# Cutting the tail of a streaming row-maximum into loads of graded size

## The chip, the cores and the metric

The kernel runs on one core of one Trainium2 chip. One execution in profile gives a span that is about 1.8 us shorter than its time (628.1 against 629.88 us for the kernel before).

## The reference

For each row of an 8192 x 8192 float32 matrix, the largest absolute value:

```python
def setup_inputs():
    return {"x": np.random.randn(8192, 8192).astype(np.float32)}

def reference(x):
    return np.linalg.norm(x, ord=np.inf, axis=1)
```

The input is 268.4 MB and the output 32 KB. Every element is read once and compared once, so the kernel is a stream from DRAM into on-chip memory with one reduction behind it.

## The kernel before

The rows are spread over 128 partitions, 64 rows to a partition. The first 48 rows are the bulk: 24 loads of two rows (16,384 columns, 8.4 MB) into three rotating buffers, each followed by one VectorE reduction. The last 16 rows are the tail: eight buffers of two rows, cut into smaller loads so that the reduction behind the last byte is short.

```python
TAIL = (
    [[8192]] * 8
    + [[4096, 4096]] * 5
    + [[2048] * 4] * 2
    + [[2048, 2048, 2048, 1024, 512, 512]]
)
# ...
    for a in range(A):                       # bulk
        for n in range(G):
            t = sbuf.tile([P, B * cols + 16], F32, tag="t")
            nc.sync.dma_start(out=t[:, : B * cols], in_=x_b[a, n])
            absmax(r_bulk[:, a, n * B : (n + 1) * B], ...)
    nc.scalar.dma_start(out=out_b, in_=r_bulk[:])      # the bulk store
# ...
            for k, w in enumerate(TAIL[r]):  # tail, row by row
                nc.sync.dma_start(
                    out=t[:, at : at + w], in_=x_t[i // B][:, at : at + w]
                )
                # ... one absmax per load, into part[:, r, k] or behind the buffer
```

All loads are issued by SyncE. The last load's reduction reads its own columns and, behind them in the buffer, the partial results of the last row (517 columns in all); its result goes out with the last small DMA.

## Time and profile before

| Kernel before | value |
|---|---|
| time, median | 629.97 us (three runs: 629.9 to 630.3; with three more 630.14) |
| input stream | 427 GB/s over the span, 434 GB/s in the bulk (loads of 8.4 MB land 19.28 to 19.37 us apart, 19.33 in the mean) |
| last bulk tile landed / its reduction ended | 467.46 / 484.7 us |
| last byte landed | 623.50 us |
| VectorE ended | 625.74 us, 2.23 us after the last byte |
| rest (result DMA, closing barrier) | 2.36 us |

The groups of instructions of the kernel before (page part 5: busy us, mean ns of one | idle before it, and what ended that):

```profile
L63 DVE TENSOR_REDUCE r_bulk<-t 128x2 f32<-128x16384 f32 x24 | 413.3, 17219 | 70.5 <-DMA t<-in_x_dram 70.5
L63 DVE TENSOR_REDUCE part<-t 128x1 f32<-128x4096 f32 (+2 forms) x26 | 130.0, 5067 | 1.3 <-DMA t<-in_x_dram 1.3
...
L63 DVE TENSOR_REDUCE r_fin<-t 128x1 f32<-128x517 f32 x1 | 0.7, 692 | 0.0
```

In the bulk VectorE waits 70.5 us for loads (17.22 us of work per 19.33 us of stream). In the tail it waits only 1.3 us before the 26 of its 32 reductions that this line counts (1.7 us in all): it comes in 17 us behind, because it may begin the last bulk tile only when that has landed, and has to catch up. It can, but slowly: a column costs VectorE 1.0416 ns (reductions of 8,192 and 4,096 columns start 8.60 and 4.33 us apart), and the stream brings one every 1.19 ns (loads of 8,192 columns land 9.72 us apart).

The end of the kernel before in the timeline (start us, us, engine, line, operation, output<-input, count, in brackets the idle time before it):

```profile
615.96 0.22 DVE L63 TENSOR_REDUCE r_tail<-part 128x15 f32<-128x60 f32 x1
616.09 2.28 DVE L63 TENSOR_REDUCE t<-t 128x1 f32<-128x2048 f32 x1
616.21 0.35 ACTq L88 DMA_DIRECT2D out_dram<-r_tail  x1
618.52 2.29 DVE L63 TENSOR_REDUCE t<-t 128x1 f32<-128x2048 f32 x1 [0.15 <-DMA t<-in_x_dram]
621.01 4.01 DVE L63 TENSOR_REDUCE t<-t 128x1 f32<-128x2048 f32 x3 [0.20 <-DMA t<-in_x_dram]
625.05 0.69 DVE L63 TENSOR_REDUCE r_fin<-t 128x1 f32<-128x517 f32 x1
625.77 0.35 SPq L99 DMA_DIRECT2D out_dram<-r_fin  x1
```

VectorE waits for the last load of 2,048 columns until 621.01. The bytes behind it (1,024 + 512 + 512 columns) are all there by 623.50, but from 621.01 VectorE still has 2,048 + 1,024 + 512 + 517 columns to reduce and is done at 625.74. So here the small last load does not make a short end, because a load three places before it is large.

Last, SyncE's own waits and one DMA line of the kernel before (us in total, times, longest; then KB and us from issue to landing):

```profile
SPq L82 <- DMA t<-in_x_dram: 65.5, 21, 4.6
...
SPq L82 <- DMA out_dram<-r_bulk: 23.2, 1, 23.2
```

```profile
out_dram<-r_bulk ACTq DMA_DIRECT2D x1, 24.0 KB, 57.9
```

A load is carried by 16 DMA engines, eight packets each, and sends one completion from each of them (the trace has 128 packets and 16 completions for each load); "ring" means the row of packets of one queue on one engine. The loads share eight rotating semaphores with the other DMAs (numbers 100 to 107 in the trace), so each waits for the DMA eight places before it. One of those is the store of the bulk result: 24 KB, but 57.9 us from issue to landing. One load waits 23.2 us for it. That costs nothing here, since the stream still has loads queued: the store lands at 542.66 us, and the loads issued by then last to 550.06.

### The profile page before, as it was taken

How to read it: one execution, taken by the hardware profiler on the slowest of the kernel's cores; microseconds unless marked ns; L12 is line 12 of the kernel's file. 1: busy time of each engine (PE TensorE's matmuls, PEld its weight loads, DVE VectorE, ACT ScalarE, POOL GpSimd, SP SyncE). 2: the span in 40 equal slices, each digit the busy share in tenths (PEclk: the TensorE clock that was granted, in tenths of full speed). 3: DMA queues.
4: the chain of work that ended last, by engine and by line, in shares of the span. 5: the costliest groups of instructions: out<-in, count | busy, mean ns of one | idle time of the engine just before them, and what ended most of it. 6: DMA issues, size and time to landing. Idle time of an engine off the chain costs nothing.

```text
span 628.1 us, 196 instructions
## 1 busy us (share of the span) xinstructions
DVE 552.7 (88%) x58; POOL 0.2 (0%) x4
## 2 busy tenths in 40 slices
DVE  0588988889988889888898888998889999999998
POOL 0000000000000000000000000000000000000000
DMA  9999999999999999999999999999999999999996
GB/s 401 413 455 413 455 413 455 413 455 413 455 413 455 409 459 413 455 413 455 413 455 413 455 413 455 413 455 413 455 405 430 434 435 432 420 432 432 424 426 274
DMA packets 9138, 268.49 MB, mean 427 GB/s; under 512 B 1968, under 2 KB 1968, under 8 KB 2352
## 3 DMA queue, kind: packets, MB, share of 16 engines
q1 hardware_dynamic: 8208, 268.44, 99.1%
q10 hardware_dynamic: 928, 0.03, 0.1%
q14 instruction: 2, 0.02, 0.0%
HBM read 268.44 MB, written 0.03 MB: 427 GB/s over the span
## 4 chain that ended last, share of the span: by engine, by line
DMA 64%; DVE 30%; another core or an unknown queue 4%; issue 1%; SPq 0%
DMA t<-in_x_dram 64%; DVE r_bulk L63 23%; DVE part L63 5%; DVE t L63 1%; SPq L82 0%; DVE r_fin L63 0%; SPq L68 0%
## 5 line engine op out<-in xcount | busy, mean ns | idle before, releaser
L63 DVE TENSOR_REDUCE r_bulk<-t 128x2 f32<-128x16384 f32 x24 | 413.3, 17219 | 70.5 <-DMA t<-in_x_dram 70.5
L63 DVE TENSOR_REDUCE part<-t 128x1 f32<-128x4096 f32 (+2 forms) x26 | 130.0, 5067 | 1.3 <-DMA t<-in_x_dram 1.3
L63 DVE TENSOR_REDUCE t<-t 128x1 f32<-128x2048 f32 (+2 forms) x5 | 8.6, 1746 | 0.4 <-DMA t<-in_x_dram 0.4
L60 DVE MEMSET part<- 128x60 f32 x1 | 0.1, 108 | 0.8 <-PEq L114 0.8
L63 DVE TENSOR_REDUCE r_fin<-t 128x1 f32<-128x517 f32 x1 | 0.7, 692 | 0.0
L63 DVE TENSOR_REDUCE r_tail<-part 128x15 f32<-128x60 f32 x1 | 0.2, 216 | 0.0
L114 POOL MEMSET const-bfloat16-1.0<- 128x1 bf16 x1 | 0.1, 101 | 0.0
L114 POOL MEMSET const-uint8-127<- 128x1 uint8 x1 | 0.1, 101 | 0.0
L114 POOL MEMSET const-float32-0.0<- 128x1 f32 x1 | 0.1, 98 | 0.2 <-issue 0.2
L114 POOL MEMSET const-float32-1.0<- 128x1 f32 x1 | 0.1, 98 | 0.0
## 6 DMA issues: line engine op xcount, KB each, us to landing
t<-in_x_dram SPq DMA_DIRECT2D x8, 4096.0 KB, 37.0
t<-in_x_dram SPq DMA_DIRECT2D x10, 2048.0 KB, 30.4
t<-in_x_dram SPq DMA_DIRECT2D x11, 1024.0 KB, 24.6
t<-in_x_dram SPq DMA_DIRECT2D x1, 512.0 KB, 15.9
t<-in_x_dram SPq DMA_DIRECT2D x2, 256.0 KB, 13.2
t<-in_x_dram SPq DMA_DIRECT2D x24, 40.7
out_dram<-r_bulk ACTq DMA_DIRECT2D x1, 24.0 KB, 57.9
out_dram<-r_tail ACTq DMA_DIRECT2D x1, 7.5 KB, 5.6
```

The source lines that it names most:

```text
L60: nc.vector.memset(part[:], 0.0)
L63: nc.vector.reduce_max(out=o, in_=i, axis=X, apply_absolute_value=True)
L114: nc = _bacc.Bacc("TRN2", target_bir_lowering=False, num_devices=1)
```

## The change

The tail is cut into loads of graded size. In the last two buffers each is mostly 0.83 to 0.95 of the one before it; in the earlier ones large and small loads mix (those of each buffer add up to 16,384 columns). A load may span the boundary of two rows (its two pieces are then reduced separately). The ratio to aim at is 0.88, the quotient of VectorE's and the stream's time per column (1.0416 and 1.19 ns): each load should be reduced just while the next arrives, down to a last load of 1,024 columns. Core of the diff:

```diff
-TAIL = (
-    [[8192]] * 8
-    + [[4096, 4096]] * 5
-    + [[2048] * 4] * 2
-    + [[2048, 2048, 2048, 1024, 512, 512]]
-)
+TAIL = [
+    [2944, 13440],
+    [4096, 12288],
+    [11520, 4864],
+    [7680, 8704],
+    [6528, 3328, 6528],
+    [4864, 4096, 3328, 4096],
+    [3968, 3584, 3328, 2944, 2560],
+    [2432, 2176, 1920, 1664, 1536, 1280, 1152, 1024, 1152, 1024, 1024],
+]
# ... segments() cuts each load at the row boundary; the loop now goes load by load:
+        for j, w in enumerate(loads):
+            nc.sync.dma_start(out=t[:, at : at + w], in_=x_t[i][:, at : at + w])
+            at += w
+            for _, b, c, n in [s for s in todo if s[0] == j]:
+                # ... absmax of this piece, as before
```

Loads in the tail go from 32 to 31, reductions on loaded data from 32 to 38. Bulk, buffers and bytes stay.

More of the change, by code (lines that the diff above doesn't have):

```diff
@@ L13, with segments @@
 X = mybir.AxisListType.X
-TAIL = (
-    [[8192]] * 8
-    + [[4096, 4096]] * 5
-    + [[2048] * 4] * 2
-    + [[2048, 2048, 2048, 1024, 512, 512]]
-)
+TAIL = [
[8 more added lines that the diff above has]
+]
+def segments(loads, cols):
+    out, at = [], 0
+    for i, w in enumerate(loads):
+        end = at + w
+        while at < end:
+            r = at // cols
+            to = min(end, (r + 1) * cols)
+            out.append((i, r, at - r * cols, to - at))
+            at = to
+    return out
 @with_exitstack
@@ L33 @@
     BUFS: int = 3,
+    PAD: int = 16,
 ):
@@ L37 @@
     rows, cols = x.shape
-    n_tail = len(TAIL)
-    assert n_tail % B == 0
+    W = B * cols
+    n_tail = B * len(TAIL)
     n_bulk_rows = rows // P - n_tail
@@ L52 @@
     outp = ctx.enter_context(tc.tile_pool(name="outp", bufs=1))
-    k_last = len(TAIL[-1])
+    segs = [segments(loads, cols) for loads in TAIL]
+    count = {}
+    for i, s in enumerate(segs):
+        for _, r, _, _ in s:
+            count[i * B + r] = count.get(i * B + r, 0) + 1
+    n_last = count[n_tail - 1]
+    k_max = max(count[r] for r in range(n_tail - 1))
+    assert n_last - 1 <= PAD
     r_bulk = outp.tile([P, A, G * B], F32)
@@ L57 @@
     r_fin = outp.tile([P, 1], F32)
-    k_max = max(len(r) for r in TAIL[:-1])
     part = outp.tile([P, n_tail - 1, k_max], F32)
@@ L66 @@
         for n in range(G):
-            t = sbuf.tile([P, B * cols + 16], F32, tag="t")
-            nc.sync.dma_start(out=t[:, : B * cols], in_=x_b[a, n])
+            t = sbuf.tile([P, W + PAD], F32, tag="t")
+            nc.sync.dma_start(out=t[:, :W], in_=x_b[a, n])
             absmax(
                 r_bulk[:, a, n * B : (n + 1) * B],
-                t[:, : B * cols].rearrange("p (b c) -> p b c", b=B),
+                t[:, :W].rearrange("p (b c) -> p b c", b=B),
             )
     nc.scalar.dma_start(out=out_b, in_=r_bulk[:])
-    for i in range(0, n_tail, B):
-        t = sbuf.tile([P, B * cols + 16], F32, tag="t")
-        for j in range(B):
-            r = i + j
-            at = j * cols
-            last = r == n_tail - 1
-            for k, w in enumerate(TAIL[r]):
-                nc.sync.dma_start(
-                    out=t[:, at : at + w], in_=x_t[i // B][:, at : at + w]
-                )
-                if last and k == k_last - 1:
-                    absmax(r_tail[:, : n_tail - 1], part[:])
-                    nc.scalar.dma_start(
-                        out=out_t[:, : n_tail - 1], in_=r_tail[:, : n_tail - 1]
-                    )
-                    absmax(r_fin[:], t[:, at : B * cols + k_last - 1])
-                elif last:
-                    absmax(
-                        t[:, B * cols + k : B * cols + k + 1], t[:, at : at + w]
-                    )
-                else:
-                    absmax(part[:, r, k : k + 1], t[:, at : at + w])
-                at += w
@@ new lines @@
+    seen = {}
+    for i, loads in enumerate(TAIL):
+        t = sbuf.tile([P, W + PAD], F32, tag="t")
+        todo = segs[i]
+        at = 0
+        for j, w in enumerate(loads):
+            nc.sync.dma_start(out=t[:, at : at + w], in_=x_t[i][:, at : at + w])
+            at += w
+            for _, b, c, n in [s for s in todo if s[0] == j]:
+                r = i * B + b
+                k = seen.get(r, 0)
+                seen[r] = k + 1
+                lo = b * cols + c
+                if r < n_tail - 1:
+                    absmax(part[:, r, k : k + 1], t[:, lo : lo + n])
+                    if r == n_tail - 2 and k == count[r] - 1:
+                        absmax(r_tail[:, : n_tail - 1], part[:])
+                        nc.scalar.dma_start(
+                            out=out_t[:, : n_tail - 1], in_=r_tail[:, : n_tail - 1]
+                        )
+                elif k < n_last - 1:
+                    absmax(t[:, W + k : W + k + 1], t[:, lo : lo + n])
+                else:
+                    absmax(r_fin[:], t[:, lo : W + n_last - 1])
```

## The prediction

> **What bounds the kernel now.** The input stream. The page gives 268.4 MB at 427 GB/s; the DMA row is 9 in 39 of 40 slices. In the trace, loads of 16,384 columns land 19.37 us apart (433 GB/s) and tail loads of 8,192 every 9.72 us. [...] So only what follows the last byte can go.
>
> **The end of before (timeline).** The last bulk tile lands at 467.46 us and its 17.22 us reduction ends at 484.6, so VectorE enters the tail 17 us behind. Reductions of 8,192, 4,096 and 2,048 columns start 8.60, 4.33 and 2.20 us apart: 1.0416 ns a column plus about 0.06 us. The stream brings a column every 1.19 ns, so VectorE gains 12% and just catches up over the 156 us of the tail (idle there: 1.7 us). The last landings: 620.98 (2,048 columns), 622.27 (1,024), 622.90 and 623.50 (512 each). VectorE does 2,048, 1,024, 512 and 517 columns after 620.98 and ends at 625.74, 2.24 us after the last byte. The result's DMA and the barrier take 2.36 us more.
>
> **What the change does.** Bulk, bytes and buffers stay. Tail loads go from 32 to 31, reductions in the tail from 32 to 38 (loads that span rows need two): 6 x 0.06 = 0.4 us more VectorE work. The ratio 0.88 is the two rates' quotient (1.0416/1.19 = 0.875): each load is reduced just while the next arrives. With the trace's rates I get landings of the last three loads (1,152, 1,024, 1,024) at about 621.1, 622.3 and 623.5, VectorE starting the last at 623.6 and ending at about 624.8. The same sum for before gives 625.6 (measured 625.74).
>
> Stream: a packet costs about 8 ns plus its bytes (8 KB 309 ns, 32 KB 1213 ns, 64 KB 2418 ns), so other sizes cost it nothing.
>
> **Issue waits.** Eight load semaphores rotate, and one slot is held by the bulk result's store, which takes 57.9 us: 48 small packets per ring, each apparently alternating with one load packet (48 x 1.21 = 58). [...] After the change I expect it to land near 543 again, with the stream filled to about 553: no bubble. Later loads wait for the eighth before, with about 10 us of stream left.
>
> **On the critical path:** only the end after the last byte, 2.24 us to about 1.3 us. That is 0.9 us, 0.15%.
>
> **Predicted:** 629.1 us, 8 in 10 between 628.5 and 629.9. Faster by over 2%: 0.003; within 2%: 0.992; slower: 0.005.
>
> **What would show each step.** Last byte at 623.5 +- 0.4 from the span's start; VectorE ends 1.2 to 1.5 us after it; r_fin's reduction reads about 1,034 columns and is busy 1.2 us; VectorE idles about 1.2 us in the tail, mostly before the 12,288 and 11,520 loads; the bulk store takes 55 to 60 us and the stream has no hole after it.
>
> **What would make it wrong.** Loads of odd widths (11,776 or 53,760 bytes a row) streaming slower than 27 bytes/ns per engine: 1% over the tail is 1.6 us, more than the gain. VectorE not having caught up at the end because early large loads make it wait longer than I sum. Or a store landing 10 us later, which would drain the stream.

## More of the kernel before

The metric is the device time of one execution in microseconds (us), the median of the fast runs.

The page of the kernel before, parts 2 and 3 (in the DMA row a digit is the busy share of one of 40 slices in tenths; a queue's line has packets, MB and its share of the 16 engines' time):

```profile
DMA  9999999999999999999999999999999999999996
...
DMA packets 9138, 268.49 MB, mean 427 GB/s; under 512 B 1968, under 2 KB 1968, under 8 KB 2352
...
q1 hardware_dynamic: 8208, 268.44, 99.1%
...
q14 instruction: 2, 0.02, 0.0%
```

The stream is busy in every slice but the last: it is what bounds the kernel.

## The result, and the profile after

| | before | after |
|---|---|---|
| time, median of 6 runs | 630.14 us (629.9 to 630.55) | 629.40 us (629.15 to 629.86) |
| last bulk tile landed | 467.46 us | 467.59 us |
| last byte landed | 623.50 us | 623.99 us |
| stream from last bulk tile to last byte | 156.04 us | 156.40 us |
| VectorE ended | 625.74 us | 625.42 us |
| ... after the last byte | 2.23 us | 1.43 us |
| rest | 2.36 us | 2.29 us |
| span of the profiled run | 628.1 us | 627.7 us |

The ratio is 0.9988 with a 95% interval of 0.9975 to 1.0001: the same within 2%, and the times alone do not settle that it is faster. (A ratio is the mean time of one kernel's runs over that of the other's of the same rounds, so it is not quite the ratio of the medians quoted. Executions over 1.5% slower than the fastest of the same kernel are left out of the means.) The traces tell more than the times here, and they show two things that go against each other: the end after the last byte became 0.80 us shorter, and the last byte came 0.49 us later.

The page of the kernel after, the lines that answer to those of before:

```profile
DMA packets 8994, 268.49 MB, mean 428 GB/s; under 512 B 1952, under 2 KB 1952, under 8 KB 3104
...
q14 instruction: 2, 0.02, 0.0%
...
L88 DVE TENSOR_REDUCE part<-t 128x1 f32<-128x8192 f32 (+18 forms) x31 | 130.4, 4273 | 0.9 <-DMA t<-in_x_dram 0.6
L88 DVE TENSOR_REDUCE t<-t 128x1 f32<-128x1152 f32 (+3 forms) x6 | 7.9, 1386 | 0.0
L88 DVE TENSOR_REDUCE r_fin<-t 128x1 f32<-128x1030 f32 x1 | 1.2, 1225 | 0.0
```

The end of the kernel after in the timeline:

```profile
614.21 1.88 DVE L88 TENSOR_REDUCE part<-t 128x1 f32<-128x1664 f32 x1
616.12 0.22 DVE L88 TENSOR_REDUCE r_tail<-part 128x15 f32<-128x60 f32 x1
616.25 7.91 DVE L88 TENSOR_REDUCE t<-t 128x1 f32<-128x1536 f32 x6
...
624.19 1.23 DVE L88 TENSOR_REDUCE r_fin<-t 128x1 f32<-128x1030 f32 x1
625.44 0.35 SPq L126 DMA_DIRECT2D out_dram<-r_fin  x1
```

No bracket stands behind any of these lines: VectorE works without a visible pause to the end, and only one reduction of 1,030 columns (1.23 us) lies behind the last byte, where before there was a piece of a large one and three small ones. The bulk store and the wait for it (SyncE's waits, then the DMA line):

```profile
SPq L106 <- DMA out_dram<-r_bulk: 25.0, 1, 25.0
```

```profile
out_dram<-r_bulk ACTq DMA_DIRECT2D x1, 24.0 KB, 60.0
```

The store lands at 544.9 us, the loads queued by then last to 553.0 us, so no hole opens.

Where did the 0.49 us of the last byte come from? 0.13 us were there when the tail began. In the tail, landing by landing, the rest is made up by one step: the load of 4,096 columns that ends the sixth tail buffer took 5.31 us to land after the one before it, where such a load took 4.80 to 4.98 us in the kernel before. The packet records of the trace show why that load is late: one of its 128 packets of 16,384 bytes took 1,251 ns, where their median is 611 ns. Right before it, at 579.58 us, an 8,192-byte packet of the instruction queue (q14) had taken 309 ns, and the slow packet began at its end, at 579.89. The same happens once more at 593.62 us (a packet of 912 ns where the median is 498), but no load lands late there. In the kernel before, one such pair lies in the stream (588.35 us), and the second q14 packet comes only at 626.95, when the stream is over.

The late load also reaches the end. Lines of the timeline of the kernel after, then of the chain of work that ended last (start us, us, what):

```profile
520.12 95.96 DVE L88 TENSOR_REDUCE part<-t 128x1 f32<-128x8192 f32 x25 [0.64 <-DMA t<-in_x_dram]
```

```profile
556.97 40.73 DMA t<-in_x_dram
597.70 0.02 issue
597.72 18.37 DVE part L88 x8
```

VectorE's one long wait is that of 0.64 us. But its reductions at 589.43, 593.73 and 597.72 also begin within 0.03 us of a landing, after waits that are too short for a bracket, and the chain runs over the stream up to the landing at 597.70. Reductions that wait for nothing overlap by 0.08 us in this trace; measured by that, the three waits add up to about 0.4 us (an estimate), nearly the 0.44 us by which the load that landed at 584.66 us was late (5.31 us less the 4.87 of the mean such load in the kernel before).

### The profile page after: what moved, and what is told of

The parts are those of the page before. It is cut to its first block, busy times and chain, and to the rows that moved or that the text cites. A ratio compares the mean times of both kernels' runs of the same rounds, so it can differ in the third digit from the quotient of the medians.

```text
span 627.7 us, 201 instructions
## 1 busy us (share of the span) xinstructions
DVE 553.0 (88%) x64; POOL 0.2 (0%) x4
## 4 chain that ended last, share of the span: by engine, by line
DMA 67%; DVE 28%; another core or an unknown queue 4%; SPq 0%; issue 0%
DMA t<-in_x_dram 67%; DVE r_bulk L88 22%; DVE part L88 5%; DVE t L88 1%; DVE r_fin L88 0%; SPq L106 0%; SPq L93 0%; DVE r_tail L88 0%
## 5 line engine op out<-in xcount | busy, mean ns | idle before, releaser
L88 DVE TENSOR_REDUCE part<-t 128x1 f32<-128x8192 f32 (+18 forms) x31 | 130.4, 4273 | 0.9 <-DMA t<-in_x_dram 0.6
L88 DVE TENSOR_REDUCE t<-t 128x1 f32<-128x1152 f32 (+3 forms) x6 | 7.9, 1386 | 0.0
```

Source lines behind the costliest of these rows:

```text
L88: nc.vector.reduce_max(out=o, in_=i, axis=X, apply_absolute_value=True)
```

## The experiments

Two questions. First, what makes the end after the last byte: the sizes in the last tail buffer alone, the grading of the whole tail, or only the size of the last load? Second, what delays the last byte: the unequal sizes, or the instruction queue's packets, and is there any danger from the bulk store? Each kernel is the changed kernel with one edit, except where "the tail of before" is named (its sizes written in the changed kernel's table). All gave the correct result. The four sessions were on four chips, and each ran the kernel before alongside; its median was 629.87 to 630.42 us. The table has the profiled run of each; "fetches" counts 8-KB packets of the instruction queue between the span's start and the last byte.

| kernel | last bulk tile to last byte | VectorE's end after last byte | fetches | span of that run | time, median |
|---|---|---|---|---|---|
| before | 156.04 | 2.23 | 1 | 628.10 | 630.14 |
| after | 156.40 | 1.43 | 2 | 627.71 | 629.40 |
| after_again | 156.53 | 1.44 | 2 | 628.47 | 629.48 |
| last_only | 156.30 | 1.72 | 1 | 628.36 | 629.53 |
| first_seven | 156.35 | 2.21 | 2 | 628.43 | 630.02 |
| unaligned | 156.99 | 1.28 | 2 | 628.54 | 629.92 |
| fine_end | 156.50 | 1.48 | 2 | 627.86 | 629.49 |
| more_code | 156.22 | 1.48 | 10 | 632.38 | 633.78 |
| store_two | 159.28 | 1.44 | 2 | 630.75 | 632.36 |
| store_small | 161.16 | 1.43 | 2 | 632.50 | 634.28 (one run) |
| before_more | 156.47 | 2.20 | 2 | 628.60 | 630.36 |
| rows_graded | 156.04 | 1.73 | 1 | 627.60 | 629.81 |
| two_issuers | 156.06 | 1.75 | 0 | 630.32 | 632.53 |
| rows_better | 156.70 | 1.45 | 1 | 628.03 | 629.81 |

### The change again (after_again)

No edit.

> The changed kernel as it is, to see what repeats. Theory A (the gain is the shorter end after the last byte, and single slow packets in the stream take part of it back at random): VectorE again ends 1.2 to 1.5 us after the last landing, against 2.24 us before; the load of 4,096 columns that took 5.31 us at 579 to 585 us takes 4.87 us this time; time 0.5 to 1.0 us below the kernel before. Rival (the unequal loads themselves stream slower at that place): the same load takes about 5.3 us again.

The end after the last byte repeated (1.44 us). But my theory of the day, that the late load was chance, fell: the same load was late again (last byte of that buffer 20.12 us after the one before it, 19.96 the first time, 19.54 in the kernel before), again with one packet of 16,384 bytes at 1,260 ns, behind a packet of the instruction queue. The load is late for a reason that is in the program. The rival, that the sizes themselves stream slower there, was still open. Time 629.48 against 629.87 us of the kernel before, 0.4 us less where 0.5 to 1.0 was expected; the ratio of 0.9995 (0.9982 to 1.0007) does not show that it is less.

### Only the last tail buffer graded (last_only), only the first seven (first_seven)

```diff
 # last_only: seven buffers as before, then
+    [2432, 2176, 1920, 1664, 1536, 1280, 1152, 1024, 1152, 1024, 1024],
 # first_seven: seven graded buffers, then
+    [2048, 2048, 2048, 2048, 2048, 2048, 2048, 1024, 512, 512],
```

> Seven tail tiles as before, only the last tile cut in the graded way (11 loads from 2,432 to 1,024). Theory A: what the grading of the last tile alone gives is the whole gain. In the trace of before VectorE starts the last tile at 607.07 us, in that after the change at 607.22, so from there it should end at 625.3 us, 1.2 to 1.6 us after the last byte, time 0.5 to 1.0 us below before. Rival (the grading has to run through the whole tail for VectorE to be caught up): VectorE enters the last tile late and ends 2 us or more after the last byte, no gain.

> The graded loads in the first seven tail tiles, the last tile as before (2,048 x 7, 1,024, 512, 512). Theory A: VectorE ends 2.1 to 2.4 us after the last byte as before, time within 0.3 us of before. Rival (whole grading): most of the gain is here, 1.2 to 1.6 us after the last byte, 0.5 us or more faster.

The end after the last byte is 2.23 us with neither, 2.21 with the first seven alone, 1.72 with the last alone and 1.43 with both. So the grading of the first seven buffers gains nothing by itself, the last buffer gives 0.5 of the 0.8 us, and the other 0.3 us need both. Theory A of last_only was right in direction but too strong: it asked for at most 1.6, and for a time 0.5 to 1.0 us below before, where 0.3 was measured. The reason is in VectorE's pauses: in the tail it idles 1.62 us in last_only and 0.96 us in the changed kernel, where it waits for loads of 8,192 and 4,096 columns in the middle of the tail. Theory A of first_seven held (2.21 us; time 0.15 us above before). The times point the same way: 629.53 us for last_only, 630.02 for first_seven, against 629.87 for the kernel before (intervals 0.9984 to 1.0009 and 0.9989 to 1.0016, so the order among them is shown by the traces and not by the times).

### A finer end (fine_end)

```diff
-    [2432, 2176, 1920, 1664, 1536, 1280, 1152, 1024, 1152, 1024, 1024],
+    [2432, 2176, 1920, 1664, 1536, 1280, 1152, 1024, 896, 768, 640, 512, 384],
```

> The changed kernel with the last eight loads cut finer (896, 768, 640, 512, 384 in place of 1,152, 1,024, 1,024; 13 loads in the last tile for 11). Theory G (VectorE works without a pause from the landing of the 11,520 load at 520 us on, so its whole remaining work sets the end, and each further load adds 0.06 us to it): VectorE ends 0.1 to 0.2 us later than with the change, 140.7 to 141.0 us after it began the tail, and time is the same within 0.3 us. Rival (what follows the last byte is the last load's own reduction): the end after the last byte falls from 1.43 us to about 0.6 us and the time by 0.7 us.

The rival is refuted: it asked for about 0.6 us after the last byte. Theory G held in its numbers, though not in its reason. The last reduction is now much shorter (its group in the page of fine_end):

```profile
L88 DVE TENSOR_REDUCE r_fin<-t 128x1 f32<-128x392 f32 x1 | 0.6, 561 | 0.0
```

Yet VectorE ends 1.48 us after the last byte (1.43 with the change), 140.82 us after it began the tail (140.67 and 140.81), and the time is 629.49 us. (The 0.1 to 0.2 us that Theory G asked for two more loads are no more than two runs of the change differ by, so that cost is not shown.) VectorE is not without a pause from 520 us on, as the theory had it: its last wait of note ends with the landing at 597.70 us in the changed kernel and at 597.52 in fine_end. From there to 625.42 us (625.36) it is fed without a visible gap, so what sets its end is all the work it has left at that landing, and a smaller last load only moves where it is queued. Grading and VectorE's rate are one limit: with 12% to spare, no load may be larger than about 14% of the columns that follow it (an estimate from the two measured rates, 1.19/1.0416 - 1, which no run tests by itself), apart from what one lets stand at the end.

### Boundaries off the grid (unaligned)

```diff
-    [2944, 13440],
+    [2977, 13407],
 # ... likewise +33/-33 columns in every tail buffer
```

> The changed kernel with nearly all inner load boundaries moved by 33 columns (132 bytes), so that neither the rows in DRAM nor those in SBUF start on a multiple of 256 bytes. Theory A (a packet costs about 8 ns plus its bytes whatever its size and start): stream and time as in after_again within 0.3 us. [...]

The stream of the tail took 156.99 us against 156.40 and 156.53, so 0.5 us more; time 629.92 us, 0.4 us more. That is over the 0.3 us of Theory A, so it did not hold as it stands. The packets show little: where the changed kernel's 13,312-byte packets had a median of 498 ns, here they had 500, and those of 16,004 to 16,516 bytes took 604 to 616. That is up to 3 ns more for most sizes, 8 for the worst. So starts on the grid are worth keeping here, but for half a microsecond. It also answers the rival of after_again in part: sizes and starts matter far less than the one late packet of 0.6 us.

### More code on an idle engine (more_code)

```diff
+    idle = outp.tile([P, 1], F32)
+    for _ in range(1024):
+        nc.gpsimd.memset(idle[:], 0.0)
```

> The changed kernel with 1,024 one-column memsets on the idle GpSimd engine at its start (about 100 ns each, nobody waits for them). It tests what the runs so far suggest: in every trace the one late packet of a slow tail load begins right after an 8,192-byte packet of the instruction queue, at the same instruction each time. Theory F (each instruction fetch of 8 KB takes its place in one ring of the 16, puts that ring about 0.7 us behind for the rest of the stream, and the last byte waits for the slowest ring): the instruction queue shows 7 to 9 packets more inside the span, the last byte comes 0.7 us (all on different rings) to 6 us (all on one ring) after 624.3, and the time follows. Rival (fetches are hidden, the late loads have another cause): last byte at 624.0 to 624.7 us as in the changed kernel, time within 0.3 us of it.

633.78 us, 4.3 us slower than the change, ratio to the kernel before 1.0063 (1.0051 to 1.0076). The page of more_code:

```profile
POOL 6666666666100000000000000000000000000000
...
DMA packets 9002, 268.55 MB, mean 425 GB/s; under 512 B 1952, under 2 KB 1952, under 8 KB 3104
...
q14 instruction: 10, 0.08, 0.0%
```

Eight packets of the instruction queue more, one for about every 127 memsets. The packet records show what each does:

```
q14 packet at (us)   took (ns)   next packet of 65,536 bytes on that ring took (ns; usual 2,418)
 12.17               309         2,632
 32.03               309         2,762
 52.00               309         2,771
 72.00               309         2,771
 91.99               309         2,760
111.96               309         2,771
131.96               309         2,771
151.95               309         2,762
```

Each fetch sets its ring back by 309 + about 350 ns, together 0.66 us, and while they go on the loads land 19.96 to 20.00 us apart, where it is 19.28 to 19.37 us in the kernel before. The last bulk tile landed at 472.09 us, 4.5 us later than with the change: seven of the eight delays show, while the load of the first fetch landed at 22.82 us, as in the kernel before (22.80). The delays add up, so they fall on one and the same ring, and a load has landed only when its slowest ring is done: its first of 16 completions now comes 5.5 us before its last, where it comes 0.5 to 1.1 us before it in the tails of the kernels before and after. It is not the memsets: of the packets of that size after the first 20 us, 2,939 took the usual time and 7 did not, and each of those 7 stands behind a fetch.

The tail of more_code took only 156.22 us although two more fetches fell into it, at 584.45 and 597.88 us (packets of 1,156 ns after the one, of 853 after the other). The late ring had not caught up: the first completion of each load stays 5.5 to 5.7 us before its last down to the last load. So these two fetches lie on rings with time to spare, and not on the late ring, where each would have delayed the landings by 0.7 to 0.9 us more (309 ns and the 408 to 564 ns by which the next packet was slow). A fetch cost time where its ring was the slowest (seven of the first eight here, 4.5 us together) or became so (the late load of the changed kernel, 0.44 us: its first completion came 1.08 us before its last, that of the load before it 0.67).

### The bulk store in two (store_two) and beside small loads (store_small)

```diff
 # store_two
-    nc.scalar.dma_start(out=out_b, in_=r_bulk[:])
+    h = G * B // 2
+    for s in (slice(0, h), slice(h, 2 * h)):
+        nc.scalar.dma_start(out=out_b[:, :, s], in_=r_bulk[:, :, s])
 # store_small: the first four tail buffers
+    [2048, 2048, 2048, 2048, 2048, 2048, 2048, 2048],   # x4
```

> The changed kernel with the bulk result stored in two halves by two DMAs, each again 48 packets a ring (16 bytes each). Theory S (each small packet of the store waits for one load packet of its ring, and the load that comes eight DMAs later waits for the store): the first store starts two bulk tiles earlier, crawls through 64 KB packets and lands near 520 us, the second near 550 to 556; each holds back a load until the stream has run dry, so SyncE waits for them, the stream shows two holes of about 2 us, and the last byte and time come 3 to 5 us later than with the change. Rival (small writes to DRAM are slow by themselves, about 1.2 us each): each store takes 58 us wherever it is, the first lands near 504, the second near 562, and the holes add up to 8 us or more. Third outcome: no hole, time unchanged: then the semaphore wait is not what matters.

> The first four tail tiles are cut into loads of 2,048 columns (8 KB packets, 0.309 us each) in place of 2 loads each; the rest as in the change. Theory S (packet by packet in turn): the bulk store's 48 packets a ring then take 48 x 0.309 = 15 us, so it lands 15 to 19 us after it was issued, not 58 to 60. Rival (the store is slow by itself): 55 to 60 us again. The time is only a look: within 1 us of the change.

The DMA line of store_small, then that of store_two:

```profile
out_dram<-r_bulk ACTq DMA_DIRECT2D x1, 24.0 KB, 15.2
```

```profile
out_dram<-r_bulk ACTq DMA_DIRECT2D x2, 12.0 KB, 68.5
```

Beside 8-KB load packets the same store takes 15.2 us, as 48 x 0.309 us says, beside 32-KB ones 57.9: it advances by one of its 48 small packets a ring for each load packet. Theory S holds, and the rival (small writes are slow as such) is refuted.

In store_two I had expected two holes and found one. The first half landed at 514.7 us, before the stream had run dry, and cost nothing. The second landed at 553.33, just after the last queued load (553.16), and the next load landed 6.8 us later where its 3,328 columns need 4.0. The SyncE waits of store_two, and its timeline there:

```profile
SPq L108 <- DMA out_dram<-r_bulk: 62.9, 2, 33.4
```

```profile
553.34 43.67 SPq L108 DMA_DIRECT2D t<-in_x_dram  x16
567.71 24.37 DVE L88 TENSOR_REDUCE part<-t 128x1 f32<-128x6528 f32 x6 [2.50 <-DMA t<-in_x_dram]
```

One hole of 2.8 us, and the time is 632.36 us, 2.9 us slower than the change (3 to 5 were expected, for two holes). store_small has such a hole too: the store landed at 499.89, the last queued load at 499.72, the next at 504.69 instead of 502.2. So a small store really can drain the stream, through the semaphore it holds. The changed kernel escapes by 8 us of queued loads (544.9 to 553.0). store_small shows besides that small loads cost by their number: its loads of 2,048 columns land 2.49 us apart, a buffer of eight in 19.88 us instead of 19.42, in line with 8 ns for each packet. With the hole, the smaller loads and two fetches close together (520.89 and 523.70 us) its single run took 634.28 us, 4.9 more than the change, where I had expected at most 1 us of difference.

### The tail of before with more VectorE instructions (before_more)

```diff
+    for _ in range(8):
+        nc.vector.memset(idle[:], 0.0)      # at the start; the tail's loads as in before
```

> The tail of before (same 32 loads, same 32 reductions), with eight one-column memsets more on VectorE at the start, so that VectorE runs 74 instructions, as many as in the runs that fetch twice, in place of 66. Theory F2 (with more instructions VectorE's program crosses into another 8 KB block, which is fetched inside the tail and sets one ring of the stream back): both packets of the instruction queue lie before the last byte, the second near 594 to 597 us; the last byte comes at 623.8 to 624.4, 0.3 to 0.7 us later than in before, and the time is 0.3 to 0.7 us longer. Rival (the later last byte of the change comes from the loads' sizes): second packet still near the end, last byte at 623.5, time equal.

Theory F2 holds in what counts: the loads and reductions of before, and yet the second fetch is now in the stream (568.68 us; I had said 594 to 597), the tail takes 156.47 us (156.04), and the last byte comes at 624.04, 0.54 us later. The time is 630.36 against 629.93 us of before in that session; the interval of the ratio (0.9992 to 1.0016) does not separate them, so this rests on the trace. There the load in flight at 568.68 us, 4,096 columns as in before, takes 5.34 us to land, its neighbours 4.84 to 4.91. So the later last byte comes without any change in the loads' sizes, and in rows_graded below the sizes change and it does not come.

The records do not say whose instructions a packet holds. By count, one always comes after SyncE has begun 79 or 80 of its instructions. The other comes when VectorE has begun 45 to 47, in the kernels in which VectorE has 71 or more in the profile; where it has 66 or 67, the second packet is found only at 625 us or later. In two_issuers, where SyncE has 72, none lies in the stream. That it is VectorE's program reaching into one more 8-KB block is therefore inferred. The two fetches do not weigh the same. In the seven kernels of the table that have both in the tail and no code on GpSimd or small loads (after to before_more), the load in flight at VectorE's fetch lands 0.4 to 0.6 us late, and at SyncE's, which is the later one there, the landings that follow shift by about 0.1 us or less.

### A graded tail with few instructions (rows_graded, two_issuers, rows_better)

```diff
 # rows_graded and two_issuers
+    [8192, 8192],                      # x4
+    [4096, 4096, 4096, 4096],          # x2
+    [4096, 4096, 3072, 2688, 2432],
+    [2304, 2176, 1920, 1792, 1664, 1536, 1280, 1152, 1024, 768, 768],
 # two_issuers besides
-            nc.sync.dma_start(out=t[:, :W], in_=x_b[a, n])
+            issuer = nc.scalar if a < 4 else nc.sync
+            issuer.dma_start(out=t[:, :W], in_=x_b[a, n])
 # rows_better: the last two buffers
+    [3072, 2688, 2432, 2944, 2688, 2560],
+    [2304, 2176, 1920, 1792, 1664, 1536, 1280, 1152, 1024, 896, 640],
```

> A tail graded without loads that span rows: 8,192 x 8, 4,096 x 10, then 3,072 down to 768; 32 loads, 32 reductions, 66 VectorE instructions as in before. Theory F2: the instruction queue has only one packet inside the stream, the last byte comes at 623.5 to 623.8, VectorE ends 1.2 to 1.7 us after it, time 0.6 to 1.1 us below before, 0 to 0.4 us below the change. Rival (the spanning loads matter): the end after the last byte stays over 2 us as in before.

> The same tail as rows_graded, with the first 16 of the 24 bulk loads issued by ScalarE, so that no engine's program reaches the next 8 KB block within the stream. Theory F2: no packet of the instruction queue inside the stream; last byte 0 to 0.7 us earlier than in rows_graded (623.0 to 623.6), time 0 to 0.7 us lower, the lowest of all kernels. Rival: the hand-over between the two issuing engines opens a hole or the fetches weigh nothing: last byte at 623.6 or later.

> A tail worked out from what the runs showed: no load spans two rows, 33 loads and 33 reductions (67 VectorE instructions, so still one instruction fetch inside the stream), from 8,192 x 8 and 4,096 x 8 down to 896 and 640, with the steps of rows 12 and 13 finer than in rows_graded. Theory: the stream of before (last byte 623.4 to 623.7 us, 156.0 to 156.3 us after the last bulk tile) together with the short end of the change (VectorE ends 1.3 to 1.5 us after the last byte, 1.73 in rows_graded): VectorE's end at 624.9 to 625.1 against 625.42 with the change, span 627.2 to 627.5, time 0.6 to 1.1 us below before. Rival: with fewer reductions VectorE is not caught up, end 1.7 us or more after the last byte; or 67 instructions already bring the second fetch and the last byte is at 624.0.

rows_graded did nearly what was expected in the trace: one fetch, last byte at 623.51, tail 156.04 us as in before, VectorE 1.73 us after it (1.2 to 1.7 expected), and with 627.60 us the shortest span of any profiled run. Its times are no better than the change's and missed the 0.6 to 1.1 us that were expected (629.81 against 629.93 us of before; 0.9983 to 1.0007).

two_issuers failed for another reason. Its timeline at the hand-over:

```profile
332.05 51.47 DVE L88 TENSOR_REDUCE r_bulk<-t 128x2 f32<-128x16384 f32 x3 [21.42 <-DMA t<-in_x_dram]
```

The last bulk load of ScalarE and the first of SyncE ran side by side and landed together, at 332.02 and 332.20 us instead of 19 us apart. Both buffers then were full at once, none came free before 349.3, and while the load in flight landed at 351.4, the next came only at 373.5, 22.1 us later instead of 19.3: a hole of 2.8 us, and 632.53 us (630.87 to 633.87). The run still tells something. With no fetch in the stream its tail took 156.06 us, with SyncE's alone (rows_graded, same loads) 156.04. So SyncE's fetch is hidden here, and it is VectorE's that shows. My expectation that taking SyncE's away would gain up to 0.7 us was wrong. It looks as if SyncE's fetches fall on a ring that is ahead of the slowest one by about one fetch (the first of a load's 16 completions comes 0.7 to 0.9 us before the last in rows_graded and before); which ring it is, the records don't say.

rows_better should have joined both gains and did not in its profiled run: VectorE ended 1.45 us after the last byte as meant, with one fetch, but the last byte came at 624.16. At 490.4 us eight packets at once had each taken 0.5 to 0.9 us too long, with no fetch near, and that buffer landed 0.3 us late; the buffer with the fetch took 19.98 us, against 19.70 in rows_graded. Its times, 629.81 against 630.42 us of before in that session, ratio 0.9991 (0.9977 to 1.0004), are those of the change. I hand on no version as better than the changed kernel.

## Why the prediction was right

The time was predicted at 629.1 us, 628.5 to 629.9, and measured at 629.4. It was right, for mostly the right reason, with one step that failed and was small. The number itself tests little: the range reaches to the 629.9 us of the fastest runs of the kernel before.

- **What bounds the kernel: right.** The last byte came at 623.5 to 625.0 us in all kernels without a hole and without code on GpSimd, and none of the edits to the tail made the stream from the last bulk tile to the last byte shorter than in before.
- **The end after the last byte: right, slightly mis-sized.** "2.24 us to about 1.3 us"; measured 2.23 to 1.43. r_fin read 1,030 columns in 1.23 us (said: about 1,034 and 1.2). VectorE began the last reduction 0.2 us after the last byte, where the prediction had 0.1. It idled 0.96 us in the tail (said: 1.2), most of it, 0.64 us, before the load of 11,520 columns.
- **The stream: the step that failed.** "Last byte at 623.5 +- 0.4", and "other sizes cost it nothing"; measured 623.99, and 623.88 to 624.62 in the three other runs with the same first seven buffers and neither a hole nor code on GpSimd. The term that was left out of the sum is not a size at all. Six more reductions make VectorE's program longer, and with that length a second instruction fetch falls within the stream (shown by before_more; whose program it is, is inferred). It costs 0.3 to 0.5 us here (tails of 156.35 to 156.53 us with two fetches against 156.04 in the kernel before), and VectorE's waits at 589 to 598 us hand it on to the end. My own first theory for it, chance, fell with after_again.
- **The added VectorE work: right.** Six reductions more were put at 0.4 us; VectorE's work in the tail, without its idle time, grew from 139.38 to 139.71 us. It stays hidden in time VectorE would have waited (0.8 us less idle time in the tail).
- **The issue waits: right, and confirmed.** Predicted 55 to 60 us for the bulk store and no hole; measured 60.0 and none. The turn-taking was put as apparent; store_small shows it (15.2 us beside 8-KB packets, 48 x 0.309), and store_two shows that the danger named ("a store landing 10 us later, which would drain the stream") is real.
- **Odd widths: right to fear them little.** 0.5 us when nothing is aligned, in unaligned.
- **Net.** Predicted 0.9 us of gain; the profiled spans give 0.4, the medians of the first session 0.7, those of the second 0.4. Of the 0.8 us gained at the end, 0.4 to 0.5 went to the stream. The scatter of single runs of the change (629.15 to 630.24 in 11) is as large as the gain, so nobody should tell these two kernels apart by two or three times.

What stays open: why SyncE's fetch, when it is the only one, is hidden in some runs (before and rows_graded, 156.04 us) and not wholly in another (last_only, 156.30), which rings take the fetches, and what made eight packets slow at once in rows_better (156.70 with one fetch). Nothing was found that removes the fetches and leaves the rest alone.

## What to carry to other kernels

When a stream bounds a kernel and the engine behind it is only some per cent faster, look for the last load that this engine has to wait for: here the end after the last byte was set by the work left at that landing (in the kernel before 2,048 columns and as many again behind them), and a smaller last load alone gained nothing (fine_end). The ratio of the two rates is a guide to the cut; stop where the extra instructions cost as much as they save (six more reductions cost 0.33 us of VectorE here). Look at every queue that shares the DMA rings with the stream, however few its bytes: a 24-KB store crept along with the loads for 60 us and held a semaphore all the while, and an 8-KB instruction fetch cost 0.66 us of one ring or more, for which the loads then waited where that ring was the slowest (19.96 to 20.00 us apart in more_code, 19.33 in the kernel before). Before a gain of a tenth of a per cent is put down to a cause, read it from landings and packets in the trace and repeat the run.
